# A transformer encoder layer on one Trainium2 core: the order of fetches, stores and operand loads in branch B

## The chip, the cores and the metric

The kernel runs on one core of a Trainium2 chip. Its engines work side by side, each through its own list of instructions in order: TensorE (PE; its weight loads are shown as PEld), VectorE (DVE), ScalarE (ACT), GpSimd (POOL) and SyncE (SP). SyncE does nothing but issue transfers (DMAs); ScalarE and GpSimd issue some too. An instruction that has to wait holds up everything behind it in its engine's list. The metric is the device time in microseconds (us) of one execution, the median over several runs. Before the change it is 2152.05 us (2150.76 to 2152.45, three runs).

## The reference

One encoder layer with two token mixers in parallel, on two sequences: a prompt of 1024 tokens and a sample of 512, model width 1024, all in 32-bit floats.

```python
xn = rmsnorm(x)
z  = xn @ W_in        # q_A k_A v_A | q_B k_B v_B | gate_A gate_B
o_A = gqa_attention(rope(norm(q_A)), rope(norm(k_A)), v_A)     # 8 heads, 2 kv heads
o_B = neighbourhood_attention(q_B, k_B, v_B, bias)             # 8 heads, 8 x 16 window on a grid
mix = (sigmoid(gate_A) * (o_A @ W_pA) + sigmoid(gate_B) * (o_B @ W_pB)) @ W_out
x = x + mix
x = x + relu(rmsnorm(x) @ W_up)**2 @ W_down
y = rmsnorm(x)
```

Tokens lie on a grid that is 64 wide. In branch B a query sees a window of 8 rows by 16 columns, with a learned bias for each relative position.

## The kernel before

**Numbers.** Each matrix product is done as three (helper `mm3`): an operand is split into a high part `hi`, rounded to the matmul's format, and a low part `lo = x - hi`, and hi*hi + hi*lo + lo*hi are summed. So a loaded operand first goes through a *split* (`split`, L192 and on): a copy on ScalarE for `hi` (L199), a subtraction on VectorE for `lo` (L206).

**Stages.** The sample (512 tokens, `NB` = 1) goes through the token mixer first, then the prompt (1024 tokens, `NB` = 2), then both through the MLP. A mixer has branch A (attention), branch B (`phB`, L905 and on) and phase G, which projects branch B and applies W_out. The *long branch B* is that of the prompt; in the profile it lies between 776 and 1070 us.

**Branch B in units.** A unit is one head and one quarter of the grid's columns: 8 heads x 4 = `n` = 32 units. The loop at L1166 runs over `i`; in iteration `i` it traces

- `s_unit` of unit `i`: scores on TensorE (`sb`), bias and row minimum on VectorE (L1031), exp on ScalarE into a tile `pb` (L1057, two such tiles in the long branch), the scaling on GpSimd (L1060). Between sums and exp it traces `turn` of unit `i-1`;
- the loads for later: `prep_bias` (L926), `prep_v` (L935; *strips* of the value matrix, `vs`), `load_qk` (L245);
- in iterations with `i % 8` = 6 and 7 the projection `qkproj` of the next two heads, which is evacuated by L971 and L973 (`qB`) and L991 and L993 (`kB`);
- five or eight steps of other TensorE work (`fill.pull`): at first the products of gate B (`gate`, L433), later projection A (`proj_a`, L867);
- `t_unit` of the unit three behind and `v_unit` of the unit four behind.

**The detour.** The probabilities have to be transposed before the product with the values. In the first 24 units of the long branch (`moved`) TensorE doesn't do it. `turn` (L1064) transposes 32 x 32 blocks on VectorE (L1069), GpSimd stores the tile to memory (`tb<-pb`, L1071), and `fetch_t` (L1073) has SyncE fetch it back with the blocks in their new places (`bh<-tb`, L1080, four transfers a unit, three `bh` tiles in turn). `t_unit` splits the fetched tile (ScalarE L1091, VectorE L1092), and `v_unit` (L1112) multiplies it with the strips (`ob`); `finish_o` copies the result out (L464, L465, L478) and puts it into memory (`obd`). Other units are transposed by TensorE (L1101).

**Gates.** `gate` computes 16 tiles in the long branch B, each of eight steps. A tanh on ScalarE (L454) writes one of two buffers `sg`, and a store takes it to memory (`zg`, L455). `store[0]` is ScalarE's queue; in the long branch B it is SyncE's.

**Projection A.** `proj_a` loads the first weights and the output of branch A (`load_o`: `rawo`, L846; three raw buffers) and leaves their splits in the list `oa_held`, from which the loop takes them. The weights go to a slot that the inputs `x` occupy until their last use.

**What sets the order.** The kernel is written for a planner that gives each engine its list. It starts from the order in which the program traces the instructions and from its own model of when each is ready, gives tiles their places and adds all waits. `keep_in_program_order` pins an instruction behind the one traced before it on its engine; all matmuls of the long branch B are pinned so. `note` remembers an instruction, and a block under `behind` puts what it traces behind those remembered on that engine: the score sums behind splits on VectorE, the exps behind splits on ScalarE, the fetches and strips behind loads on SyncE. The block empties the list.

Of the kernel before, what the change touches and what calls it, by code (L numbers as in the profile page):

```python
# [11 lines left out]
F32 = mybir.dt.float32  # L12
# [6 lines left out]
P = 128  # L19
# [42 lines left out]
def encoder(ctx: ExitStack, tc: tile.TileContext, xs, outs, w):  # L62
# [123 lines left out]
    def note(engine, op):  # L186
        if held_pe:
            firm[engine].append(op.ins)
# [230 lines left out]
    def run(tr, nxt, first):  # L419
# [7 lines left out]
        oad = dram.tile([4 * P, T], F32, name=f"oad{N}")  # L427
        obd = dram.tile([4 * P, T], F32, name=f"obd{N}")
        fill = Fill()
        store = [nc.scalar]  # L430
        later_put = []

        def gate(goff, dst, c0=0, c1=NC8):  # L433

            nxt_w = load_cols(win, goff + c0 * P, P, f"g{N}_{goff}_{c0}")
            yield
            for c in range(c0, c1):
                wg = nxt_w
                held = []
                if c + 1 < c1:  # L440
                    nxt_w = load_cols(win, goff + (c + 1) * P, P, f"g{N}_{goff}_{c + 1}", hold=held)
                for tb in range(NB):
                    nm = f"{N}_{goff}_{c}_{tb}"
                    g_ = mm(f"gps{nm}")
                    for k in range(NC8):
                        mm3(g_, wg[k][0], wg[k][1], xh(tb, k), xl(tb, k), k == 0, k == NC8 - 1)
                        if k + 1 < NC8:
                            yield
                        if k == 2:
                            while held:  # L450
# [3 lines left out]
                    nc.scalar.activation(sg, g_, AF.Tanh, scale=0.5)  # L454
                    store[0].dma_start(dst[c * P : (c + 1) * P, tb * 512 : tb * 512 + 512], sg)  # L455
                    yield

        def finish_o(o, n, dst, pool, nm, parts=None):

            t = pool.tile([HD, 512], F32, tag="ot", name=f"ot_{nm}", bufs=1)  # L460
            if len(o.shape) == 3:

                tv = t[:, : 2 * n].rearrange("p (i q) -> p i q", i=2)
                nc.scalar.activation(tv, o[HD:P], AF.Copy)  # L464
# [4 lines left out]
            n_os = 2  # L469
            if parts is not None:  # L470
                hi, lo, ps = parts
                b = pool.tile([P, n], F32, tag="os", name=f"os_{nm}", bufs=n_os)[ps, :n]
# [4 lines left out]
            b = pool.tile([HD, n], F32, tag="os", name=f"os_{nm}", bufs=n_os)  # L477
            nc.vector.tensor_tensor(b[:, :n], o[0:HD, :n], t[:, :n], op=ALU.add)  # L478
            if store[0] is nc.scalar:
                nc.scalar.dma_start(dst, b[:, :n])  # L480
            else:
                later_put.append((dst, b[:, :n]))


        def load_a(g, between=None, then=None, last=None):
# [353 lines left out]
        def load_o(br, hold=None, raw_of=raw_tile):  # L839
            parts = []  # L840
            for k in range(4 - br):
                t = slot([P, 2, T], F32R, f"oX{N}_{br}_{k}", first and br + k == 0)

                def ask(k=k, t=t):
                    raw = raw_of(f"rawo{N}_{br}_{k}")
                    note("SP", nc.sync.dma_start(raw[:, :T], (oad, obd)[br][k * P : (k + 1) * P, :]))  # L846
                    return partial(split, t[:, 0, :], t[:, 1, :], raw[:, :T])

                if hold is None:
                    ask()()  # L850
                elif NB == 1 or k < 2:
                    hold.append(ask())
                else:

                    cuts = []
                    early = hold[k - 2]

                    def then(early=early, ask=ask, cuts=cuts):
                        early()
                        cuts.append(ask())  # L860
# [45 lines left out]
        with phase(f"phB{N}") as ph:  # L906
# [41 lines left out]
            def qkproj(pr, wqk, dest):  # L948
# [4 lines left out]
                for tb in range(NB):  # L953
                    cs = slice(tb * 512, tb * 512 + 512)
                    pq = mm(f"pqb{N}_{pr}_{tb}")
                    for k in range(NC8):
                        mm3(pq, wq[k][0], wq[k][1], xh(tb, k), xl(tb, k), k == 0, k == NC8 - 1)
                        yield
                    for e in range(2):
                        hs = slice(64 * e, 64 * e + 64)  # L960
                        ls = slice(64 - 64 * e, 128 - 64 * e)

                        src = pq[hs].rearrange("p (r j c) -> p j r c", j=4, c=16)

                        def strip_view(s_):
                            return qT[s_, e, :].rearrange("p (j r c) -> p j r c", j=4, c=16)[
                                :, :, tb * 8 : tb * 8 + 8, :
                            ]

                        dst_h, dst_l = strip_view(hs), strip_view(ls)  # L970
                        nc.scalar.activation(dst_h, src, AF.Copy, scale=0.125)  # L971
                        for jj in range(4):
                            nc.vector.scalar_tensor_tensor(  # L973
                                dst_l[:, jj],
                                src[:, jj],
                                0.125,
                                dst_h[:, jj].bitcast(F32),
                                op0=ALU.mult,
                                op1=ALU.subtract,
                            )  # L980
# [174 lines left out]
            qp = None  # L1155
            held = []
            if moved:
                store[0] = nc.sync
                held_pe.append(1)
                fill.pull(3)  # L1160
            due_t, due_v = {}, {}
            for i, u in enumerate(units):
                ls = 3 if u in moved else 3 - NB
                due_t.setdefault(i + ls, []).append(u)
                due_v.setdefault(i + ls + 1, []).append(u)
            for i in range(n + 4 - NB):  # L1166
                if i < n - 8:
                    f = (5 if i < 2 else 2 + i % 2) if NB == 1 else 5 - (i % 6 == 5)
                else:
                    f = 3 + i % 2 if NB == 1 else 8  # L1170
                if NB == 2 and i == n - 10:
                    pa = proj_a(ph, raw_here)
                    next(pa)
                if i < n:
                    late = i > 0 and units[i - 1] in moved
                    s_unit(units[i], partial(turn, units[i - 1]) if late else None)
                    h, j = units[i]
                    if j == 1 and h < 7:
                        if moved:
# [40 lines left out]
                fill.pull(f - f // 2)  # L1220
                for u in due_v.get(i, ()):
                    v_unit(u)
                if 0 < i <= n and units[i - 1] in moved:
                    fetch_t(units[i - 1])
                if NB == 2 and oa_held and i >= n - 9:
                    oa_held.pop(0)()
                while len(later_put) > (i < n):
                    nc.sync.dma_start(*later_put.pop(0))
            fill.drain()
            held_pe.clear()  # L1230


        mgs = {}
# [713 lines left out]
```

## Time and profile before

| | |
|---|---|
| median of 3 runs | 2152.05 us |
| profiled execution | 2149.47 us |
| its span, first to last instruction | 2147.7 us |
| mean granted clock of TensorE | 0.995 |
| TensorE busy | 2104.3 us (98%) |
| VectorE busy | 1486.6 us (69%) |
| ScalarE busy | 1141.4 us (53%) |
| GpSimd busy | 368.6 us (17%) |
| long branch B, 776 to 1070 us: TensorE busy | 279.88 of 294.00 us, clock 0.98 |

The profile lists instructions by kernel line, engine and tile name, as `out<-in`. A view of waits says who waited for whom: total, number, longest. The chain of waits follows the last instruction back to what released it; "issue" there is idle time for which the profile shows no cause. A timeline row has start, duration, engine, line, operation, and in brackets the idle time before it with what ended it. In rows by stage stand, behind the length, the busy time of PE, PEld, DVE, ACT and POOL with the number of instructions, then the granted clock (1.00 is full), the share of the DMA engines' time in use, and GB/s.

### The profile page before, as it was taken

The numbers are of one execution on the slowest core, as the hardware profiler recorded it, in microseconds if no ns is written. First come the engines' busy times: TensorE is split into PE (matmuls) and PEld (weight loads), VectorE is DVE, ScalarE is ACT, GpSimd is POOL, SyncE is SP. The second block draws the span as 40 slices with busy tenths as digits, with TensorE's granted clock in tenths as the row PEclk, the third lists the DMA queues.
The fourth block names the chain that finished last, engine by engine and source line by source line (L and its number), as shares of the span: only waits on it lengthen the run. The fifth ranks groups of instructions, "written<-read, shape, count | busy, mean of one in ns | idle before, by whom it ended". The sixth has DMA issues, their size and how long they took to land.

```text
span 2147.7 us, 32028 instructions
## 1 busy us (share of the span) xinstructions
PE 2104.3 (98%) x10871; PEld 1840.9 (86%) x10871; DVE 1486.6 (69%) x2793; ACT 1141.4 (53%) x2487; POOL 368.6 (17%) x470
## 2 busy tenths in 40 slices
PE   9999999999999999989999999999999999999998
PEld 8888778888897888777888899999999988888886
DVE  6665786767657757766882877778777777759662
ACT  6664653767656645544540566566655643334442
POOL 2232310323232214533200200003000000000000
PEclk9999999999999999999999999999999999999999
DMA  6437557520122136667572665578545799788561
GB/s 192 131 101 209 154 151 251 185 77 25 52 81 70 42 96 191 202 187 205 174 235 103 210 199 178 177 245 206 164 142 157 253 356 342 215 271 282 167 206 59
DMA packets 337002, 372.95 MB, mean 174 GB/s; under 512 B 33471, under 2 KB 269639, under 8 KB 336839
## 3 DMA queue, kind: packets, MB, share of 16 engines
q1 hardware_dynamic: 296695, 296.17, 44.6%
q10 hardware_dynamic: 31072, 45.11, 6.0%
q0 software_dynamic: 9072, 29.63, 4.7%
q8 instruction: 86, 1.41, 0.3%
q14 instruction: 77, 0.63, 0.1%
HBM read 274.29 MB, written 97.32 MB: 173 GB/s over the span
## 4 chain that ended last, share of the span: by engine, by line
PE 65%; issue 1%; DVE 1%; DMA 1%; ACT 1%; POOL 0%; SPq 0%; POOLq 0%; ACTq 0%; DVEq 0%
PE dn L212 20%; PE ua L212 6%; PE ud L212 6%; PE uc L212 6%; PE gpss L212 5%; PE ops L212 4%; PE ub L212 3%; PE pqbs L212 2%; PE ppbs L212 2%; PE pkbs L212 2%; PE dnf L212 2%; PE ppas L212 1%; PE pTs L812 1%; PE obs L212 1%; PE sbs L212 1%
## 5 line engine op out<-in xcount | busy, mean ns | idle before, releaser
L212 PE MATMUL dn<-wd,ah 128*128 128x512 f32 x1248 | 384.3, 389 | 0.0
L212 PEld LDWEIGHTS dn<-wd,ah 128*128 128x128 f32 x1248 | 234.3, 188 | 48.4
L212 PE MATMUL dn<-wd,al 128*128 128x512 f32 x624 | 242.9, 389 | 0.0
L1421 ACT ACTIVATE ah<-ar 128x512 fp32r<-128x512 f32 x168 | 104.1, 627 | 196.6 <-PE dn L212 179.8
L212 PE MATMUL gpss<-xs_0h,w_gs 128*128 128x512 f32 x512 | 188.5, 402 | 0.7 <-DVE ot_Bs L465 0.4
L1422 DVE TENSOR_TENSOR al<-ar,ah 128x512 fp32r<-128x512 f32 x168 | 114.0, 687 | 74.3 <-ACT ah L1421 66.3
L212 PE MATMUL ud<-B,A 128*128 128x384 f32 x768 | 143.6, 335 | 0.7 <-DVE c L1539 0.7
L212 PE MATMUL uc<-B,A 128*128 128x384 f32 x768 | 143.7, 334 | 0.0
L212 PE MATMUL ua<-B,A 128*128 128x384 f32 x768 | 138.8, 334 | 0.0
L212 PEld LDWEIGHTS dn<-wd,al 128*128 128x128 f32 x624 | 117.2, 188 | 24.4
L778 POOL TENSOR_SCALAR ps<-ps,rls 128x1024 f32<-128x1024 f32 (+1 forms) x96 | 96.8, 1009 | 225.7 <-DVE rls L777 200.3
L212 PEld LDWEIGHTS ud<-B,A 128*128 128x128 f32 x768 | 133.9, 188 | 1.1 <-DVE c L1539 1.1
L212 PEld LDWEIGHTS uc<-B,A 128*128 128x128 f32 x768 | 134.1, 188 | 0.2 <-ACT A L1421 0.2
L212 PEld LDWEIGHTS ua<-B,A 128*128 128x128 f32 x768 | 133.7, 188 | 0.2
L818 DVE TENSOR_TENSOR ptls<-pTs,pths 128x512 fp32r<-128x512 f32 x160 | 107.7, 687 | 37.6 <-ACT pths L817 36.6
L817 ACT ACTIVATE pths<-pTs 128x512 fp32r<-128x512 f32 x160 | 94.1, 597 | 73.8 <-PE pTs L812 71.5
L212 PE MATMUL ops<-wh_os,mgs 128*128 128x512 f32 x384 | 119.4, 391 | 0.0
L772 DVE TENSOR_REDUCE nms<-ss 128x1 f32<-128x1024 f32 (+1 forms) x96 | 99.9, 1041 | 25.7 <-PE ss L770 25.1
L212 PEld LDWEIGHTS gpss<-xs_0h,w_gs 128*128 128x128 f32 x512 | 96.2, 189 | 18.8 <-DVE w_gs L206 0.7
L180 POOL TENSOR_TENSOR rs_f<-ms_f,mhalf 128x1 f32<-128x1 f32 x6 | 4.0, 666 | 590.7 <-DVE ms_f L176 590.7
L775 ACT ACTIVATE ps<-ss,nms 128x1024 f32<-128x1024 f32 (+1 forms) x96 | 93.2, 971 | 22.9 <-DVE nms L772 20.4
L812 PEld LDWEIGHTS pTs<-ident,ps 128*128 128x128 f32 x640 | 78.0, 140 | 28.4 <-POOL ps L778 4.3
(288 smaller groups left out, 5158.1 us busy)
## 6 DMA issues: line engine op xcount, KB each, us to landing
ar<-ud SPq DMA_DIRECT2D x120, 512.0 KB, 4.6
br<-in_w_mlp_down_dram SPq DMA_DIRECT2D x72, 512.0 KB, 5.4
rawu<-in_w_mlp_up_dram SPq DMA_DIRECT2D x64, 512.0 KB, 4.1
ud<-c ACTq DMA_DIRECT2D x128, 192.0 KB, 2.9
raw_gs<-in_w_in_dram SPq DMA_DIRECT2D x32, 512.0 KB, 3.9
ud<-cs SPq DMA_DIRECT2D x64, 192.0 KB
tbs<-pbs POOLq DMA_DIRECT2D x24, 384.0 KB, 3.5
bhs<-tbs SPq DMA_DIRECT2D x96, 96.0 KB, 2.2
```

What stands on the lines that cost most here:

```text
L180: nc.gpsimd.tensor_tensor(r[:, :n], m[:, :n], mhalf[:, :n], op=ALU.pow)
L212: op = nc.tensor.matmul(out, a, b, **kw)
L772: nc.vector.tensor_reduce(nm_, s, axis=AX.X, op=ALU.max, negate=True)
L775: nc.scalar.activation(p, s, AF.Exp, bias=nm_, accum_out=l)
L778: nc.gpsimd.tensor_scalar(p, p, rl, 1.0, op0=ALU.mult, op1=ALU.mult)
L812: nc.tensor.transpose(pt[:, j * P : (j + 1) * P], PP[u, j][:, kc * P : (kc + 1) * P], ident)
L817: nc.scalar.activation(hi, pt, AF.Copy)
L818: nc.vector.tensor_tensor(lo, pt, hi.bitcast(F32), op=ALU.subtract)
L1421: nc.scalar.activation(hi, src, AF.Copy)
L1422: nc.vector.tensor_tensor(lo, src, hi.bitcast(F32), op=ALU.subtract)
```

## The change

All of it lies in the token mixer. The stores of gate tiles and of branch B's outputs go through one function, `put`. Where `slot_no[0]` is None it issues the store on ScalarE's queue at once, as before. In the long branch B it notes the store with the number of the unit, and the loop issues it on SyncE at the end of the next unit. Before, gate stores were issued on SyncE where the tanh is traced, and of the outputs' stores the loop always kept the latest one back.

The fetch of a moved unit is traced after the scores of the unit two behind it, ahead of that iteration's strips; before, it stood at the end of the iteration that turns it, ahead of the output store.

The evacuations of `qkproj` for `qB` are noted, so sums and exps that are traced later stand behind them.

`proj_a` is begun at iteration 21 in place of 22 in the long branch; the second of the two places that take a split begins at 22 in place of 23, the first stays at 23. In the short branch the splits are taken from iteration 21 on, in place of 23. `load_o` asks for its raw tile ahead of the slot for the split.

```diff
-        store = [nc.scalar]
-        later_put = []
+        later_put, slot_no = [], [None]
+
+        def put(dst, src):
+            if slot_no[0] is None:
+                nc.scalar.dma_start(dst, src)
+            else:
+                later_put.append((slot_no[0], dst, src))
...
-                    store[0].dma_start(dst[c * P : (c + 1) * P, tb * 512 : tb * 512 + 512], sg)
+                    put(dst[c * P : (c + 1) * P, tb * 512 : tb * 512 + 512], sg)
...
-            if store[0] is nc.scalar:
-                nc.scalar.dma_start(dst, b[:, :n])
-            else:
-                later_put.append((dst, b[:, :n]))
+            put(dst, b[:, :n])
...
             for k in range(4 - br):
+                raw = None
+
+                def ask(k=k):
+                    r = raw_of(f"rawo{N}_{br}_{k}")
+                    note("SP", nc.sync.dma_start(r[:, :T], (oad, obd)[br][k * P : (k + 1) * P, :]))
+                    return r
+
+                now = hold is None or NB == 1 or k < 2
+                if now:
+                    raw = ask()
                 t = slot([P, 2, T], F32R, f"oX{N}_{br}_{k}", first and br + k == 0)
...
-                        nc.scalar.activation(dst_h, src, AF.Copy, scale=0.125)
+                        note("ACT", nc.scalar.activation(dst_h, src, AF.Copy, scale=0.125))
                         for jj in range(4):
-                            nc.vector.scalar_tensor_tensor(
+                            op = nc.vector.scalar_tensor_tensor(
...
+                            note("DVE", op)
...
             if moved:
-                store[0] = nc.sync
+                slot_no[0] = 0
...
             for i in range(n + 4 - NB):
+                if moved:
+                    slot_no[0] = i
...
-                if NB == 2 and i == n - 10:
+                if NB == 2 and i == n - 11:
                     pa = proj_a(ph, raw_here)
                     next(pa)
                 if i < n:
                     late = i > 0 and units[i - 1] in moved
                     s_unit(units[i], partial(turn, units[i - 1]) if late else None)
+                    if i > 1 and units[i - 2] in moved:
+                        fetch_t(units[i - 2])
...
-                if oa_held and i >= n - 9:
+                if oa_held and i >= (n - 9 if NB == 2 else n - 11):
                     oa_held.pop(0)()
...
-                if 0 < i <= n and units[i - 1] in moved:
-                    fetch_t(units[i - 1])
-                if NB == 2 and oa_held and i >= n - 9:
+                if NB == 2 and oa_held and i >= n - 10:
                     oa_held.pop(0)()
-                while len(later_put) > (i < n):
-                    nc.sync.dma_start(*later_put.pop(0))
+                while later_put and later_put[0][0] < i:
+                    nc.sync.dma_start(*later_put.pop(0)[1:])
             fill.drain()
             held_pe.clear()
+            slot_no[0] = None
+            for _, dst, src in later_put:
+                nc.sync.dma_start(dst, src)
```

More of the change, by code (lines that the diff above doesn't have):

```diff
@@ L468, in finish_o @@
                 nc.scalar.activation(t[:, :n], o[HD:P, :n], AF.Copy)
-            n_os = 2
             if parts is not None:
                 hi, lo, ps = parts
-                b = pool.tile([P, n], F32, tag="os", name=f"os_{nm}", bufs=n_os)[ps, :n]
+                b = pool.tile([P, n], F32, tag="os", name=f"os_{nm}", bufs=2)[ps, :n]
                 nc.vector.tensor_tensor(b, o[0:HD, :n], t[:, :n], op=ALU.add)
@@ L476, in finish_o @@
                 return
-            b = pool.tile([HD, n], F32, tag="os", name=f"os_{nm}", bufs=n_os)
+            b = pool.tile([HD, n], F32, tag="os", name=f"os_{nm}", bufs=2)
             nc.vector.tensor_tensor(b[:, :n], o[0:HD, :n], t[:, :n], op=ALU.add)
-            if store[0] is nc.scalar:
-                nc.scalar.dma_start(dst, b[:, :n])
-            else:
-                later_put.append((dst, b[:, :n]))
+            put(dst, b[:, :n])
         def load_a(g, between=None, then=None, last=None):
@@ L841, in load_o @@
             for k in range(4 - br):
+                raw = None
[6 more added lines that the diff above has]
+                    raw = ask()
                 t = slot([P, 2, T], F32R, f"oX{N}_{br}_{k}", first and br + k == 0)
[L844 to L847, printed above, removed]
+                cut = partial(split, t[:, 0, :], t[:, 1, :])
                 if hold is None:
-                    ask()()
-                elif NB == 1 or k < 2:
-                    hold.append(ask())
+                    cut(raw[:, :T])
+                elif now:
+                    hold.append(partial(cut, raw[:, :T]))
                 else:
@@ L856, in load_o, with then @@
                     early = hold[k - 2]
-                    def then(early=early, ask=ask, cuts=cuts):
+                    def then(early=early, ask=ask, cut=cut, cuts=cuts):
                         early()
-                        cuts.append(ask())
+                        cuts.append(partial(cut, ask()[:, :T]))
                     hold[k - 2] = then
```

## The prediction, made before the changed kernel ran

> **What bounds the kernel now.** I read the page first, then busy time by stage, then the waits of TensorE alone, the chain of waits, the clock in short windows, and last the queues that feed the places found.
>
> ```profile
> span 2147.7 us, 32028 instructions
> PE 2104.3 (98%) x10871; PEld 1840.9 (86%) x10871; DVE 1486.6 (69%) x2793; ACT 1141.4 (53%) x2487; POOL 368.6 (17%) x470
> ```
>
> TensorE is the bound. A change that moves other engines' work can only win where TensorE stands still or runs slowly. The change touches the neighbourhood attention (branch B) of both sequences, above all the long one, which runs from 776 to 1070 us.
>
> ```profile
> 890.00:960.00 70.00, 60.99 (x279) 50.74 (x278) 42.69 (x100) 31.71 (x62) 24.49 (x33) 0.95 0.65 189
> 960.00:1000.00 40.00, 40.00 (x194) 34.10 (x193) 29.64 (x73) 21.20 (x43) 16.93 (x23) 1.00 0.73 215
> 1000.00:1012.00 12.00, 8.62 (x27) 5.77 (x26) 8.27 (x19) 8.21 (x14) 4.22 (x4) 0.72 0.57 172
> ```
>
> The first figures are the stretch, its length and TensorE's busy time; the third from the end is the granted clock. Idle are 70.00-60.99 = 9.0 us in the first row, nothing in the second, and 12.00-8.62 = 3.4 in the third; where it idles the clock falls below 1 as well. TensorE's waits from 900 to 1010 us name the places:
>
> ```profile
> PE obs L212 <- issue: 5.5, 3, 3.2
> PE pqbs L212 <- DVE qBs L973: 3.5, 1, 3.5
> PE ppas L212 <- ACT oXs L199: 1.7, 1, 1.7
> PE ppas L212 <- DVE oXs L206: 1.6, 2, 1.2
> ```
>
> ```profile
> 943.20 3.24 issue
> ...
> 952.89 1.78 issue
> ```
>
> Place A is the 3.5 us of a projection (pqbs) at 904. Place B is 3.24 us before the value product obs at 943.20; place C is the other two waits of obs, 1.78 at 952.89 and 5.5-3.24-1.78 = 0.48. Place D is projection A (ppas) at 1001, 1.7+1.6 = 3.3 us, whose operand oX is not split yet. Each idle may also cost clock (columns as before):
>
> ```profile
> 908.48:911.90 3.42, 3.42 (x9) 2.66 (x9) 2.75 (x8) 1.69 (x4) 2.63 (x4) 0.50 0.65 179
> 946.03:949.45 3.42, 3.01 (x11) 3.04 (x12) 1.44 (x5) 1.35 (x5) 1.23 (x2) 0.50 0.85 274
> 952.86:956.27 3.41, 1.63 (x12) 1.63 (x12) 2.62 (x4) 2.61 (x4) 0.00 (x0) 1.00 1.05 275
> 1000.65:1004.06 3.41, 1.20 (x4) 0.47 (x3) 2.22 (x4) 3.39 (x5) 0.00 (x0) 1.00 0.37 110
> 1004.06:1010.88 6.82, 5.65 (x16) 3.85 (x16) 4.93 (x14) 3.54 (x9) 4.22 (x4) 0.50 0.63 191
> ```
>
> Behind A, B and D the clock is halved for 3.42, 3.42 and 6.82 us; work done in them takes twice as long, so half of the busy time there is lost: 3.42/2 = 1.7, 3.01/2 = 1.5, 5.65/2 = 2.8. The window with 3.41-1.20 = 2.21 us idle is followed by a halved one, C's own, with 3.41-1.63 = 1.78, isn't slowed, nor does the clock fall behind it. With its clock each place costs: A 3.5+1.7 = 5.2, B 3.24+1.5 = 4.7, C 2.26, D 3.3+2.8 = 6.1; 18.3 us in all, which is what there is to win.
>
> **The change part by part.** No instruction or transfer is added or dropped. It moves 96 fetches, 16 gate stores, the obd stores and some splits, and it adds order edges.
>
> *Gate stores and fetches.* SyncE issues in order. Its own waits between 800 and 1000 us, and what it did around 915:
>
> ```profile
> SPq L1080 <- DMA tbs<-pbs: 36.4, 15, 4.4
> SPq L455 <- ACT sgs L454: 23.7, 3, 14.4
> SPq L1080 <- PE obs L212: 10.5, 3, 6.2
> ```
>
> ```profile
> 924.18 0.34 SPq L455 DMA_DIRECT2D zgs<-sgs  x1
> 924.57 0.43 SPq L245 DMA_DIRECT2D raw_gs<-in_w_in_dram  x1
> 925.17 2.38 SPq L1080 DMA_DIRECT2D bhs<-tbs  x4
> 927.65 0.45 SPq L1228 DMA_DIRECT2D obds<-os_Bs  x1
> ```
>
> ```profile
> 909.76 0.57 POOL L1071 DMA_DIRECT2D tbs<-pbs  x1 [0.19 <-DVE rlbs L1059]
> ```
>
> ```profile
> DMA to landing us min/median/max: 2.6/3.5/6.6
> ```
>
> The last row is of the tbs stores. The block stored at 909.76 had landed by 909.76+6.6 = 916.4 at the latest, but its fetch went out at 925.17: a gate store sat in front of it, waiting 14.4 us for a tanh. Behind the fetch sat the obd store. What that does to B and C, on ScalarE and on VectorE:
>
> ```profile
> 940.89 0.62 ACT L1057 ACTIVATE pbs<-sbss,nmbs 128x384 f32<-128x384 f32 x1 [4.33 <-DMA tbs<-pbs]
> ...
> 942.72 0.84 ACT L1091 ACTIVATE bhs<-bhs 128x768 fp32r<-128x768 f32 x1
> ...
> 952.25 0.60 ACT L454 ACTIVATE sgs<-gpss 128x512 f32<-128x512 f32 x1 [4.85 <-PE gpss L212]
> 952.75 0.83 ACT L1091 ACTIVATE bhs<-bhs 128x768 fp32r<-128x768 f32 x1
> ```
>
> ```profile
> 933.07 0.42 DVE L478 TENSOR_TENSOR os_Bs<-ot_Bs 64x256 f32<-64x256 f32 x1 [2.44 <-DMA obds<-os_Bs]
> ```
>
> VectorE waits 2.44 us at 933.07 for an obd store to free its buffer. That holds up the score sums, so the turned block, so its landing, so the exp at 940.89 by 4.33 us; the split of the fetched block (L1091) comes only at 942.72, and that is B. In C the next split stands behind a tanh (4.85 us), which waits for TensorE, which has just come out of B.
>
> After the change a gate store is traced at the end of the unit behind its tanh, the obd store ahead of the fetch, and the fetch at the head of the next unit. In the stretch above nothing is left before the fetch that waits for TensorE: it can go at 916.4 instead of 925.17, 8.8 us sooner, and the obd store sooner still. That is more than B's 3.24 and the 4.33 behind it. I take B and C as gone: 4.7+2.26 = 7.0 us, between 0 (the split stays behind a tanh) and 7.0. Where the detour runs at its pace nothing is gained or lost by the later tracing, since the fetch waits for its store's landing there (36.4 us over 15 waits) in either order.
>
> What the move is charged with: the four fetches of a unit now stand ahead of its four strips (vss).
>
> ```profile
> 875.34 1.73 SPq L1080 DMA_DIRECT2D bhs<-tbs  x4
> ...
> 880.97 1.73 SPq L1080 DMA_DIRECT2D bhs<-tbs  x4
> ```
>
> The strips come later by 1.73 us of issue and the wait for the landing (4.4 at most), 6.1 together. A strip is used four units after its own, and a unit is 880.97-875.34 = 5.6 us here, so 22 us of other units' work cover it; without the cover it would be 6.1 us once, since all later ones are shifted alike. A gate store that is one unit late keeps one of two tanh buffers 5.6 us longer. The loop pulls five steps a unit and a gate tile has eight, so tanh come every 1.6 units and a buffer is asked for again after 3.2, 18 us; I charge nothing. Without that cover the next tanh would wait up to a unit.
>
> *Order edges.* The projection's evacuations (L971, L973) are now noted, so that sums and exps traced behind them are also issued behind them. A waits for exactly such an evacuation (L973). Gain between 0 and A's 5.2; or a loss, where a sum is held back, as large as one more wait like A's 3.5. No row shows an evacuation held up by a later exp alone, so I take 0.
>
> *Projection A's operands.* The loads are asked for one unit sooner in the long sequence, and the last splits come a unit sooner (in the short one, two).
>
> ```profile
> 991.38 1.73 SPq L1080 DMA_DIRECT2D bhs<-tbs  x4
> 993.22 0.36 SPq L846 DMA_DIRECT2D rawos<-oads  x1
> ```
>
> ```profile
> 1001.71 1.99 ACT L199 ACTIVATE oXs<-rawos 128x1024 fp32r<-128x1024 f32 x2
> ```
>
> The fourth load goes out at 993.22, behind a fetch that held SyncE up to 6.2 us for a buffer (the row of L1080 and obs above), and the splits run at 1001.71, just when TensorE wants them. A split is 1.0 us of ScalarE, which is busy 21.2 of the 40.0 us from 960 to 1000, so three fit ahead of D. Gain between 0 and 6.1, or a loss of 1.0 where a split that comes early holds up an exp. The last of four stays closest to its use, so I leave the longest wait for VectorE's part, 1.2, standing and take 6.1-1.2 = 4.9, clock included, since 1.2 is below the 1.78 that cost no clock.
>
> *The rest of the plan.* Order on every engine is worked out anew from the traced order, so small waits move. In the first sequence, where the splits come two units sooner, TensorE's longest wait in branch B is this:
>
> ```profile
> PE obs L212 <- ACT ot_Bs L464: 3.0, 1, 3.0
> ```
>
> Bounds are one wait like its 3.0 gone, and one like A's 3.5 new. I charge 1.0.
>
> **Sum.** -7.0 -4.9 +0 +1.0 = -10.9 us against the profiled execution, 2149.47 us (1.8 outside the span). The median of the runs is 2152.05, 2.6 above it; from there 2152.05-10.9 = 2141.
>
> **Rivals.**
>
> *All four places go* (0.14): A too, nothing new: 2152.05-18.3 = 2134. For: the new edges stand on the line that A waits for. Against: an edge that holds back sums and exps doesn't move the evacuation ahead of the other work in front of it, the splits of fetched blocks among it.
>
> *Only one of the two parts works* (0.14): B and C go and D's splits queue behind a tanh, 2152.05-7.0 = 2145; or only D, 2147.
>
> *D's halved clock stays* (0.04), since it hangs on something else than D's short gaps: D gives only 3.3-1.2 = 2.1 and the time is 2152.05-7.0-2.1+1.0 = 2144. Against: the window of 2.21 idle stands right before it. The Trainium skill, page "TensorE: Matmul & The Clock Gate", section "Why this matters for your kernels", has a rule of this kind: only gaps above some 3 us drop the clock. D's gaps are 1.7 at most and the clock fell all the same, so the trace disagrees with it taken as a matter of single gaps.
>
> *The change does not do what it says* (0.12): the planner issues by its own estimate of readiness, fetch and gate store end up where they were or the wait moves from one to the other; within 4 us of 2152.
>
> *Slower: the split behind the tanh becomes the rule* (0.16). A fetch traced in the later unit may be planned as landing late, and the split L1091 then goes behind that unit's tanh on ScalarE, as at 952.25, where TensorE paid 1.78 us. Sixteen gate tiles run beside the detour. From 10.9/1.78 = 6 of them on the gain is spent; ten give 2152.05-10.9+17.8 = 2159. For: the two rows at 952. Against: one of sixteen does it now, and there TensorE had just come out of B.
>
> **How the numbers follow.** The forecast has 0.40: B, C and most of D. With 0.2% (4.3 us, about what a measurement of this kernel can tell from no change) as the bound, faster holds the forecast, the full case, the half case and that of the clock, 0.72; same 0.12; slower 0.16. The range goes down to 2132, where the full case ends with 2 us of the first sequence, and up to 2154, which takes in no change and leaves out most of the slower case.
>
> **What would show it.** SyncE's wait for tanh (23.7) near 0, and the fetch after 909 out by about 916: right on the first part. TensorE's 5.5 us for obs gone and the clock at 1.00 from 940 to 960: right on B and C. Projection A with under 1.5 us of wait for oX and no halved clock at its start: right on D. A still there shows the edges idle. I am wrong if obs waits appear in many units with a tanh ahead of L1091, or if the strips become what obs waits for.

## The result, and the profile after

The changed kernel takes 2143.3 us (median of 6 runs, 2140.93 to 2144.53), the kernel before on the same chip 2150.51 (6 runs, 2148.93 to 2152.45). The ratio is 0.9964, with a 95% interval of 0.9951 to 0.9977. That is 7.7 us faster (7.2 by the medians), where 10.9 were forecast. The profiled execution took 2144.53 us, 4.9 less than the profiled one before; its span, 2142.7 us, is 5.0 shorter.

Busy time by stage for the same three stretches as before (length, then busy PE, PEld, DVE, ACT, POOL with counts, granted clock, DMA share, GB/s):

```profile
890.00:960.00 70.00, 62.48 (x289) 52.59 (x288) 44.58 (x107) 34.58 (x68) 28.29 (x38) 0.95 0.67 201
960.00:1000.00 40.00, 38.18 (x175) 32.11 (x175) 27.49 (x69) 19.19 (x38) 13.66 (x20) 0.96 0.67 189
1000.00:1012.00 12.00, 9.41 (x42) 6.76 (x41) 10.39 (x21) 7.14 (x13) 5.36 (x4) 1.00 0.51 150
```

The first stretch, which held A, B and C, idles 7.5 us (9.0 before) at the same clock of 0.95. The second, which had no idle at all, now has 1.8 and a lower clock. In the third the clock is back at 1.00. TensorE's waits from 900 to 1010 us (engine, tile, line, releaser; total, number, longest):

```profile
PE obs L212 <- issue: 6.8, 2, 4.7
PE sbs L212 <- DVE kBs L1001: 1.8, 1, 1.8
PE pqbs L212 <- DVE ot_Bs L471: 0.7, 1, 0.7
PE ppas L212 <- ACT oXs L199: 0.6, 1, 0.6
PE ppas L212 <- DVE oXs L206: 0.5, 2, 0.2
```

Against before, A has gone from 3.5 to 0.7 and D from 3.3 to 1.1, but the waits of obs (B and C) have gone from 5.5 up to 6.8, and a wait of 1.8 for kB is new. Of the three waits of obs, the first has grown from 0.48 to 2.1 and B from 3.24 to 4.7; C's 1.78 is gone. The granted clock, in its own windows:

```profile
942.30:949.13 6.83, 5.82 (x18) 5.18 (x19) 3.26 (x6) 1.84 (x4) 0.74 (x2) 0.50 0.80 226
986.68:990.09 3.41, 1.59 (x10) 1.27 (x9) 3.36 (x10) 2.21 (x6) 3.08 (x5) 1.00 0.07 29
990.09:993.50 3.41, 3.41 (x10) 2.82 (x10) 3.32 (x8) 2.40 (x6) 1.02 (x2) 0.50 0.55 171
```

Two spells of halved clock are left of three: one of 6.83 us behind B (it was 3.42) and one of 3.41 behind the new wait. Those behind A and D are gone.

**The fetches did go out sooner.** SyncE's list of after, then TensorE's, then SyncE's list of before for the next block:

```profile
918.26 1.97 SPq L1088 DMA_DIRECT2D bhs<-tbs  x4
...
926.34 1.73 SPq L1088 DMA_DIRECT2D bhs<-tbs  x4
```

```profile
917.30 0.89 PE L212 MATMUL obs<-bhs,vss 128*128 128x256 f32 x6
```

```profile
934.99 1.73 SPq L1080 DMA_DIRECT2D bhs<-tbs  x4
```

The fetch that went out at 925.17 before goes out at 918.26, the moment the obs at 917.30 ends (918.19): it waits for the `bh` tile which that product reads, one of three used in turn. The next fetch, that of the block which B's product reads, goes out at 926.34 in place of 934.99, 8.7 us sooner. B stays all the same, as the lists of ScalarE, GpSimd, VectorE and TensorE show:

```profile
935.99 0.62 ACT L1065 ACTIVATE pbs<-sbss,nmbs 128x384 f32<-128x384 f32 x1 [0.70 <-DMA tbs<-pbs]
...
937.33 0.60 ACT L460 ACTIVATE sgs<-gpss 128x512 f32<-128x512 f32 x1
940.77 0.61 ACT L1065 ACTIVATE pbs<-sbss,nmbs 128x384 f32<-128x384 f32 x1 [2.85 <-DMA tbs<-pbs]
...
941.39 0.83 ACT L1099 ACTIVATE bhs<-bhs 128x768 fp32r<-128x768 f32 x1
```

```profile
934.30 3.15 POOL L1019 TENSOR_TENSOR bms<-rects,msks 128x384 f32<-128x384 f32 x2
937.40 0.57 POOL L1079 DMA_DIRECT2D tbs<-pbs  x1
```

```profile
928.86 1.29 DVE L206 TENSOR_TENSOR w_gs<-raw_gs,w_gs 128x512 fp32r<-128x512 f32 x2 [0.27 <-ACT w_gs L199]
...
931.02 0.97 DVE L1077 STREAM_TRANSPOSE pbs<-pbs 128x768 f32<-128x768 f32 x1
...
932.23 1.09 DVE L1100 TENSOR_TENSOR bhs<-bhs 128x768 fp32r<-128x768 f32 x1
...
942.25 0.96 DVE L1100 TENSOR_TENSOR bhs<-bhs 128x768 fp32r<-128x768 f32 x1 [0.57 <-ACT bhs L1099]
```

```profile
943.31 1.62 PE L212 MATMUL obs<-bhs,vss 128*128 128x256 f32 x6 [4.68 <-issue]
```

B's product starts 0.1 us after the subtraction of its split (942.25 + 0.96 = 943.21), so it is the split that it waits for. The exp that held this split before (940.89, idle 4.33) now comes at 935.99, idle 0.70; counted from the start of the long branch, it is the 37th in both kernels. So far the change does what was forecast. But in ScalarE's list the split (L1099, 941.39) no longer stands behind that exp and a tanh alone: the planner has put the first exp of the next unit, the 39th (940.77), ahead of it. That exp waits for its `pb` tile until the store of an earlier block has landed, and that store left GpSimd at 937.40, behind the making of a bias tile (`bm`), which takes 3.15 us for its two halves. The row of the page on these fetches has a median of 2.2 us from issue to landing:

```profile
bhs<-tbs SPq DMA_DIRECT2D x96, 96.0 KB, 2.2
```

So the block was there by about 926.34 + 1.73 + 2.2 = 930.3 and lay for 11 us, at the end of which its split waited for another block's store. Ahead of that, the 2.1 us before obs at 933.5 have the same form on VectorE: the subtraction L1100 stands behind a weight split and a transposition.

### The profile page after: what moved, and what is told of

Same layout as the page of the kernel before. It is cut to its first block, busy times and chain, and to the rows that moved or that the text cites. A ratio compares the mean times of both kernels' runs of the same rounds, so it can differ in the third digit from the quotient of the medians.

```text
span 2142.7 us, 32014 instructions
## 1 busy us (share of the span) xinstructions
PE 2102.9 (98%) x10871; PEld 1841.3 (86%) x10871; DVE 1484.2 (69%) x2793; ACT 1141.0 (53%) x2487; POOL 374.0 (17%) x470
## 4 chain that ended last, share of the span: by engine, by line
PE 52%; DVE 1%; issue 0%; DMA 0%; ACT 0%; SPq 0%; POOLq 0%; POOL 0%; ACTq 0%; DVEq 0%
PE dn L212 20%; PE ua L212 6%; PE ud L212 6%; PE uc L212 6%; PE ops L212 4%; PE ub L212 3%; PE ppbs L212 2%; PE ppas L212 2%; PE dnf L212 2%; PE pt L353 0%; PE obs L212 0%; PE gpss L212 0%; PE sbs L212 0%; PE ptbs L1109 0%; DVE A L1435 0%
## 5 line engine op out<-in xcount | busy, mean ns | idle before, releaser
L780 POOL TENSOR_SCALAR ps<-ps,rls 128x1024 f32<-128x1024 f32 (+1 forms) x96 | 96.9, 1010 | 225.7 <-DVE rls L779 200.4
```

Of the source, the lines that this page charges most:

```text
L780: nc.gpsimd.tensor_scalar(p, p, rl, 1.0, op0=ALU.mult, op1=ALU.mult)
```

## The experiments

Places are named as in the prediction; times are medians, ratios are against the kernel before on the same chip, with 95% intervals.

| kernel | us | ratio |
|---|---|---|
| operands of projection A alone | 2147.75 | 0.9985 (0.9976 to 0.9994) |
| order edges of qB alone | 2150.32 | 1.0002 (0.9993 to 1.0011) |
| store lag alone | 2145.99 | 0.9981 (0.9972 to 0.9990) |
| moved fetches alone | 2147.32 | 0.9988 (0.9979 to 0.9997) |
| store lag and moved fetches | 2145.00 | 0.9974 (0.9963 to 0.9985) |
| the whole change | 2143.30 | 0.9964 (0.9951 to 0.9977) |
| whole change, four `bh` tiles | 2158.59 | 1.0043 (1.0030 to 1.0057) |
| whole change, split ahead of later exps and sums | 2138.53 | 0.9948 (0.9936 to 0.9961) |
| the same on ScalarE alone | 2140.23 | 0.9953 (0.9939 to 0.9967) |
| the same, split traced earlier | 2142.73 | 0.9971 (0.9961 to 0.9982) |
| the same, kB's evacuations noted too | 2140.17 | 0.9948 (0.9936 to 0.9961) |
| kernel before, split ahead of exps and sums | 2153.07 | 1.0007 (0.9998 to 1.0015) |

Within these intervals the parts add up: 0.9985 x 1.0002 x 0.9974 = 0.9961, the whole 0.9964.

### Projection A's operands alone

The new `load_o`, and the iterations:

```diff
-                if NB == 2 and i == n - 10:
+                if NB == 2 and i == n - 11:
...
-                if oa_held and i >= n - 9:
+                if oa_held and i >= (n - 9 if NB == 2 else n - 11):
...
-                if NB == 2 and oa_held and i >= n - 9:
+                if NB == 2 and oa_held and i >= n - 10:
```

> The kernel before with the third part alone: projection A's loads and splits sooner, nothing else. As predicted (the splits of oX came too late, and D's idle halves the clock): TensorE's wait for oX falls from 3.3 us to under 1.5, no halved clock at projection A's start, time 4 to 6 us below the kernel before. Rival (D's halved clock hangs on something else): the wait falls, the clock stays halved, 2 us. A, B and C stay as before (3.5 us and 5.5 us of wait) by both.

TensorE's waits from 890 to 1015 us:

```profile
PE pqbs L212 <- DVE qBs L978: 3.5, 1, 3.5
PE sbs L212 <- DVE kBs L998: 1.8, 1, 1.8
...
PE ppas L212 <- DVE oXs L206: 0.5, 2, 0.2
PE ppas L212 <- ACT oXs L199: 0.3, 1, 0.3
```

D's waits for oX fall from 3.3 to 0.8 and the clock from 1000 to 1012 is 1.00 (0.72 before): this part mends D by itself. It also makes the 1.8 us for kB, at once and alone, and that is one reason why it brings 3.2 us (by the ratio) and not the 4 to 6 expected. The rows of after show how: the weight split of projection A (985.55), two sums and a transposition stand ahead of kB's subtraction on VectorE.

```profile
985.55 0.76 DVE L206 TENSOR_TENSOR w_pas<-raw_pas,w_pas 128x256 fp32r<-128x256 f32 x2 [1.80 <-ACT w_pas L199]
...
988.39 1.36 DVE L1001 TENSOR_TENSOR kBs<-pkbs,kBs 64x512 fp32r<-64x512 f32 x2
```

### The order edges alone

```diff
-                        nc.scalar.activation(dst_h, src, AF.Copy, scale=0.125)
+                        note("ACT", nc.scalar.activation(dst_h, src, AF.Copy, scale=0.125))
```

and the same for the subtraction on VectorE.

> The kernel before with the second part alone: the evacuations of the branch B queries noted, so that later sums and exps stand behind them. As predicted (the edges are idle): A stays at 3.5 us with its halved clock, time within 2 us of the kernel before. Rival (A fell from 3.5 to 0.7 us in the changed kernel because of the edges): A under 1 us, no halved clock behind it, time 4 to 5 us below. B and C are not touched by either.

```profile
PE pqbs L212 <- DVE qBs L973: 3.4, 1, 3.4
PE sbs L212 <- DVE nmbs L1032: 2.6, 1, 2.6
```

The edges leave A's wait where it was, 3.4 us, and the time too. Another one appears, 2.6 us for the sums. Against the expectation A has no halved clock behind it here; the last section returns to that.

### Stores alone, fetches alone, both

The store lag is `put` with `slot_no` (the diff above). The moved fetches are:

```diff
                     s_unit(units[i], partial(turn, units[i - 1]) if late else None)
+                    if i > 1 and units[i - 2] in moved:
+                        fetch_t(units[i - 2])
...
-                if 0 < i <= n and units[i - 1] in moved:
-                    fetch_t(units[i - 1])
```

> The kernel before with the lag of the gate stores (and obd stores) alone; fetches stay at the end of the unit. The run with stores and fetches together won 5.8 us and lost A's 3.5 us of wait with its clock. If the stores did that: A under 1 us, time 4 to 6 us below the kernel before, obs waits still 5 to 7 us. If the fetches did: A at 3.5 us, time within 2 us of the kernel before.

> The kernel before with the fetches a unit later and ahead of the strips alone; gate stores stay where the tanh is. If the fetches made A's gain: A under 1 us, 4 to 6 us below. If the stores made it: A at 3.5 us and the same time. SyncE's wait for tanh stays above 15 us in either case; if it held up the fetch by itself, obs waits would be at 5.5 us or more, and the fetch near 925 would go right behind the gate store.

> The kernel before with the first part alone: gate stores one unit behind, fetches traced a unit later ahead of the strips. As predicted (the gate store ahead of the fetch makes B and C): waits for obs under 1 us, clock full from 930 to 955, time 6 to 8 us below the kernel before. Rival (the fetch is held by the third fetched tile, which the product obs three units back frees only after the projection, whatever stands before it on SyncE, and the split waits behind an exp): the fetch of the block stored near 909 us goes out when that obs ends, obs waits stay at 5 to 7 us with a halved clock, time within 2 us of the kernel before.

With the stores alone, SyncE and TensorE around the fetch that went out at 925.17 before:

```profile
911.19 0.64 SPq L245 DMA_DIRECT2D raw_gs<-in_w_in_dram  x1
926.87 1.75 SPq L1082 DMA_DIRECT2D bhs<-tbs  x4
```

```profile
925.95 0.89 PE L212 MATMUL obs<-bhs,vss 128*128 128x256 f32 x6
```

No gate store is in front of the fetch any more, and it still goes out at 926.87, 0.03 us after the end of obs (925.95 + 0.89 = 926.84). The tile held it; the gate store, which stood in front before, hid that. A stays in this kernel (4.2 us). With the fetches alone, and with both, A falls to the same 0.7 as in the changed kernel. So A hangs on where the fetch is traced. The times don't follow A alone: the stores gain 4 us with A as it was, where at most 2 had been expected, and the fetches only 2.6 with A gone, where 4 to 6 had been. Before, ScalarE copied obs out at 906.03, behind a kB copy that waited for the scores; in the changed kernel it does so at 901.50, ahead of the kB copies (902.21), and the projection begins 0.7 us after the scores:

```profile
904.07 0.59 ACT L991 ACTIVATE kBs<-pkbs 64x512 fp32r<-64x512 f32 x1 [2.96 <-PE sbs L212]
...
906.03 0.59 ACT L464 ACTIVATE ot_Bs<-obs 64x512 f32<-64x512 f32 x1
```

```profile
901.50 0.59 ACT L470 ACTIVATE ot_Bs<-obs 64x512 f32<-64x512 f32 x1 [2.52 <-PE obs L212]
```

What in the planner's reckoning turns these two round was not followed further. The waits of obs (5.5 us before) are gone in none of the three kernels: 2.7 with the stores alone, 3.5 + 1.7 = 5.2 with the fetches alone, 6.6 with both. So of the gain forecast at B and C the stores alone give about half, the fetches alone next to nothing (and a new wait of 3.2 us for sums), and together they give none. ScalarE's lists show what goes with it: with either part alone the split of B's block stays ahead of the 39th exp (942.95 against 946.12, 940.32 against 941.65), and with both it falls behind it (944.55 against 943.93), as in the changed kernel. Why the planner does so was not followed.

### Four tiles for the fetched blocks

```diff
-bufs=3)
+bufs=4)
```

for `bh`. Room for it comes from the long branch's bias tiles (`bm`, four to two), `za` (two to one) and small tiles (`sml`, eight to six).

> The changed kernel with a fourth fetched tile (room taken from bias tiles, 4 to 2 in the long branch, one za tile, small tiles 8 to 6). If the third tile, freed by the product obs, is what holds the fetch of the block stored near 909: it goes out at its landing, about 915, in place of 918.3. If that late fetch also made the obs waits, they fall by about 3 of 6.8 us and the time by 3 to 5 us; if the splits stand behind other work, the waits stay within 1 us and the time within 3 us of the changed kernel.

```profile
918.55 1.86 SPq L1088 DMA_DIRECT2D bhs<-tbs  x4
```

```profile
921.02 0.89 PE L212 MATMUL obs<-bhs,vss 128*128 128x256 f32 x6
```

```profile
PE obs L212 <- issue: 6.4, 2, 4.3
```

The fetch now leaves 3.4 us before that obs ends (921.91), where three tiles let it leave only after. The waits of obs are 6.4 us, 6.8 without. So neither this fetch nor the third tile is what B waits for. (B's own block is the next one; its fetch goes out behind the landing of its store with four tiles as with three.) The 15 us that this kernel loses against the changed one come with the room taken from the other tiles; which of these costs them was not separated.

### The split ahead of later exps and sums

On the changed kernel, the split of a fetched block is noted, so exps and sums traced later stand behind it on their engine:

```diff
-                    nc.scalar.activation(hi, lo.bitcast(F32), AF.Copy)
-                    nc.vector.tensor_tensor(lo, lo.bitcast(F32), hi.bitcast(F32), op=ALU.subtract)
+                    note("ACT", nc.scalar.activation(hi, lo.bitcast(F32), AF.Copy))
+                    note("DVE", nc.vector.tensor_tensor(lo, lo.bitcast(F32), hi.bitcast(F32), op=ALU.subtract))
```

> The changed kernel, with the splits of the fetched blocks noted too, so that the exps and sums traced behind a split are issued behind it. If B's 4.7 us in the changed kernel is a split that stands behind an exp on ScalarE, which itself waits for a stored tile to land: obs waits fall from 6.8 us to under 2, no halved clock near 942, time 6 to 9 us below the changed kernel, near 2135. If the block itself comes too late (fetch or landing): the waits stay, and exps wait behind the split as well, time the same or up to 5 us longer.

```profile
PE sbs L212 <- DVE nmbs L1039: 2.9, 1, 2.9
PE obs L212 <- issue: 2.1, 1, 2.1
```

B's 4.7 us and its 6.83 us of halved clock are gone, and of the three spells before one of 3.41 us is left. The split now runs at 935.89, ahead of the 39th exp at 939.16. So the place of the split in the lists was the cause of B. A wait of 2.9 us for sums takes part of it back. This kernel, at 2138.53 us, is clearly faster than the kernel before (0.9948). Against the changed kernel it is 4.8 us by the medians and 3.4 by the ratios; the intervals of the two overlap, but the kernel with the edge on ScalarE alone (0.9953) and the one with kB noted too (0.9948), both told of below, lie on the same side.

The same edge on ScalarE alone (the first of the two lines):

> The changed kernel with the split noted on ScalarE alone (L1099), not on VectorE (L1100). In the changed kernel the 4.68 us before obs had the split behind an exp on ScalarE, and the 2.14 us before that the subtraction behind a weight split, sums and a transposition on VectorE. If ScalarE's order is what counts, the 4.68 us are gone as with both notes and the time is about 2138.5; if VectorE's counts, it is nearer to 2143.3, that of the changed kernel.

```profile
PE obs L212 <- issue: 5.3, 2, 3.2
```

B's wait falls only from 4.7 to 3.2, with 3.4 us of halved clock, and no wait for sums appears; the time, 2140.23, can't be told from that with both. On ScalarE the split is ahead of the 39th exp (937.37 against 940.46), but on VectorE its subtraction (939.67) stands behind a transposition that first waits 0.7 us for GpSimd. So both engines' lists hold the split back.

The edge on both, and the split traced at the head of its unit:

```diff
+                    for u in due_t.get(i, ()):
+                        if u in moved:
+                            t_unit(u)
```

(ahead of the unit's scores, and left out further down)

> The kernel with the splits noted (2138.5), and the split of a fetched block traced at the head of the unit, ahead of that unit's sums and exps, in place of its middle. If the 2.14 us of obs that were left are the split's subtraction standing behind sums and the block transposition on VectorE: that wait is gone, time 2 to 4 us below, near 2135.5. If exps now wait for fetches that land late: score or obs waits appear elsewhere, 0 to 10 us above 2138.5.

```profile
PE sbs L212 <- DVE nmbs L1039: 3.8, 1, 3.8
```

That goes too far: the sums are now 3.8 us late, obs still waits 3.0 us, and the time is 2142.73.

The edge on both, and kB's evacuations (L999, L1001) noted too:

> The changed kernel with the split noted on both engines, and the evacuations of the projection for kB (L999, L1001) noted as well. The 1.82 us before the scores at 988 come from VectorE: the split of projection A's weights, two sums and a transposition stand ahead of kB's subtraction. If the edge moves those sums behind it, the 1.82 us go and the time is about 2138.5 - 1.8 = 2137; if it is the weight split that holds it up, or the sums so delayed become the next wait, it stays at 2138.5 or gets 1 to 3 us slower.

kB's 1.8 us stay: on VectorE the weight split (980.86), two sums and the transposition keep their place ahead of kB's subtraction (983.71). The edge acts on sums and exps alone, so it can't move the other two, and these sums were traced ahead of kB's evacuation.

### The same edge on the kernel before

> The kernel before, with one thing added: the splits of fetched blocks (L1091, L1092) are noted, so that sums and exps traced behind them are also issued behind them; nothing of the change is in it. If B and C hang on the place of the split in ScalarE's list, and not on when the fetch goes out, the order edge should work here too: B's 3.24 us before obs goes to under 1 with its halved clock, A and D stay, and the time is about 2150.5 - 4.7 = 2146. If the edge only helps together with the moved fetches, stores or operand loads, the 3.24 us stay or come back as a wait for sums, and the time is 2150 +- 2.

```profile
PE sbs L212 <- DVE nmbs L1031: 4.4, 1, 4.4
...
PE obs L212 <- issue: 3.4, 2, 1.8
```

```profile
956.15 1.06 ACT L199 ACTIVATE w_gs<-raw_gs 128x1024 fp32r<-128x1024 f32 x1 [5.20 <-DMA raw_gs<-in_w_in_dram]
```

B's wait falls by half here too, from 3.2 to 1.6 (the two of obs are now 1.6 and 1.8), with no halved clock behind it, but the next sums come 4.4 us late, behind a weight split for which ScalarE waits 5.2 us. What B gains here it gains on VectorE, where the subtraction (941.38) now goes ahead of the sums and the transposition. On ScalarE the edge has nothing to move: in the kernel before the split stands ahead of the 39th exp already, and the 37th, which still waits 4.2 us for a landing, is traced ahead of the split. (In the changed kernel that exp comes early, idle 0.70, so there the place of the split counts.) The load of the weight for which ScalarE waits went out at 949.72 on SyncE; in the changed kernel with the edge it went out at 944.71, and the wait for sums is 2.9. In the kernel before the edge is worth nothing, 1.0007 (the profile is of the fastest of its executions, 2148.11 us), and on the changed kernel 3 to 5 us. That the rest of the difference lies in how early SyncE gets to the weight loads fits the two rows, but was not tried by itself.

## Why the prediction was right and wrong

The time, 2143.3, lies within the range, 2.3 us from the forecast; the steps do not come out so well. Each against the profiled executions, a halved clock counted as half of the busy time in it:

| step | forecast | profiled |
|---|---|---|
| B and C | -7.0 | 7.0 before; 6.8 + 5.82/2 = 9.7 after: +2.7 |
| D | -4.9 | 6.1 before; 1.1 after: -5.0 |
| order edges, A | 0 | 5.2 before; 0.7 after: -4.5 |
| rest of the plan | +1.0 | kB 1.8 + 3.41/2 = 3.5 and w_pa 1.5 new, first sequence -1.9: +3.1 |
| sum | -10.9 | -3.7 |

The span is 5.0 shorter, so 1.3 lies in smaller waits, not followed one by one. The rows of the table aren't independent. TensorE stands ready for B's product 4.6 us sooner than before (at 943.31 - 4.68 = 938.63, before at 943.20), mostly because A and the first sequence's wait are gone, and the product starts 3.1 us sooner (946.44 before). So the 1.4 us by which B's wait has grown are gain from there handed on, and no new loss. Two rows on which the last step rests, both of after, from 900 to 1015 us and from 200 to 400:

```profile
PE ppas L212 <- DVE w_pas L206: 1.5, 1, 1.5
```

```profile
PE obs L212 <- DVE bhs L1117: 1.1, 1, 1.1
```

The first sequence's longest wait in branch B (3.0 before) is now the 1.1 of the second row.

**The step that failed** is "That is more than B's 3.24 and the 4.33 behind it. I take B and C as gone". It took the earlier fetch and output store as enough, and left the split where it stood in ScalarE's list. Half of that chain held: VectorE's wait of 2.44 us for the output store is gone, the store for which the 37th exp waits leaves 4.6 us sooner (932.44, before 937.00), and that exp comes 4.9 us sooner. But the lists were drawn up anew, and the split went behind the 39th exp, which waits 2.85 us for the next store. So the split came only 1.3 us sooner (941.39, before 942.72), and B stayed. The kernels with the noted split show it: with the split ahead of that exp, and its subtraction ahead of the transposition, B is gone.

Nor was the fetch at 925.17 that of B's block. The block stored at 909.76 is read by the obs at 938.08, which waited 0.48 us. B's block was stored and fetched later in the kernel before (the second row is SyncE's wait from 934 to 936 us):

```profile
928.21 0.59 POOL L1071 DMA_DIRECT2D tbs<-pbs  x1 [2.70 <-DVE rlbs L1059]
```

```profile
SPq L1080 <- DMA tbs<-pbs: 2.2, 1, 2.2
```

Its fetch at 934.99 waited for its own store to land, and not for a gate store. The block was there by about 934.99 + 1.73 + 2.2 = 938.9, four microseconds before its split at 942.72, and of that the prediction took no note. That this fetch came 8.7 us sooner, close to the 8.8 worked out for the other block, is chance.

Within that step, "nothing is left before the fetch that waits for TensorE: it can go at 916.4" was wrong by 1.9 us (918.26). The fetch itself waits for TensorE, by its tile. In the kernel before, the obs that frees this tile ended at 923.50 + 0.89 = 924.39, so without the gate store the fetch could have gone only 0.8 us sooner. It goes 6.9 us sooner in the changed kernel because that obs does (918.19); with the stores alone, where A stays, it goes no sooner at all (926.87). The row of the waits for obs at L1080 (10.5 us, three times) was quoted there and used only for projection A's loads.

For C the number came out, its 1.78 us is gone, but again by a change of order: the split, which stood behind the tanh at 952.25, now goes ahead of it (945.46 against 950.41).

**Order edges 0** was right, by the kernel with the edges alone (3.4 us left, 1.0002). "A still there shows the edges idle" was a bad test, for A went by another part, the moved fetches. The part on the fetches had no word on A.

**D** was right in mechanism and size: the forecast left 1.2 us at full clock, there are 1.1. The operands alone show it is this part's doing. In the changed kernel another 1.5 us for the weights of the same projection comes new and stands under the rest.

**Rest of the plan, +1.0** was too small. The bounds given, one wait of 3.0 gone and one like A's 3.5 new, were both met, together with a further 1.5. The new wait for kB belongs to the operands' part: the loss bounded there at 1.0, "where a split that comes early holds up an exp", came on VectorE instead, as a weight split ahead of an evacuation, at 3.5 with its clock.

**Of the rivals**, that the split behind other work becomes the rule came nearest to what happened at B, but at two places and not ten, and with an exp or a weight split in front, not a tanh. That the planner goes by its own estimate was true of the split, which it moved, and not of the fetch and the gate store that this rival named. The half case named 2147 for "only D"; D alone (the operands) measured 2147.75. So close a match is luck, for that 2147.75 includes the new wait for kB. What the whole has beyond D is first of all A, for which the case "all four go" had argued from the edges.

**Strips and late gate stores**, charged at nothing: strips are not among what obs waits for after. SyncE's wait for tanh fell from 23.7 us to 9.8, and to nothing for the fetch at 918.26:

```profile
SPq L1238 <- ACT sgs L460: 9.8, 3, 5.8
```

## What to carry to other kernels

Before an earlier transfer is credited with a wait, find the transfer that feeds this very instruction and look when it landed; if it lay there for microseconds, the wait belongs to the order in the list of the engine that reads it, and an order edge is what helps. Where a planner draws up the lists anew, a place in a list that a forecast rests on has to be pinned, or charged as open. Where a wait in front of a transfer is taken away, look for the next one it has, the free tile above all. And a total that comes out right says little about its terms: here a loss of 2.7 where 7.0 had been expected as gain was covered by 4.5 gained elsewhere. Part of that loss is the same 4.5 handed on, for time gained at one place is waited out again at the next if what feeds that place stays late.

## What the runs showed of the hardware

The clock doesn't follow the length of a wait, but how it falls on windows of 3.41 us. A's wait was 3.50 us before, with 3.42 us of halved clock behind it; 3.5 with the operands alone, with 6.83 behind it; and 3.44 with the edges alone, with none. Stretches of the kernel with the edges alone, and of the changed kernel with the split ahead (its 2.9 us wait lies across the two):

```profile
903.18:906.59 3.41, 1.81 (x12) 1.44 (x10) 1.06 (x2) 1.54 (x3) 1.33 (x2) 1.00 0.35 135
906.59:910.00 3.41, 1.57 (x7) 1.34 (x8) 3.35 (x11) 2.00 (x4) 0.44 (x1) 1.00 0.57 158
```

```profile
947.15:950.56 3.41, 2.21 (x13) 1.77 (x11) 1.03 (x3) 1.54 (x2) 0.00 (x0) 1.00 0.96 273
950.56:953.97 3.41, 1.73 (x8) 1.58 (x9) 3.33 (x10) 2.17 (x6) 0.57 (x1) 1.00 0.93 277
```

The windows idle 1.60 and 1.84 us in the first, 1.20 and 1.68 in the second, and the clock stays at 1.00 (there is no spell of halved clock behind either). The new wait for kB in the changed kernel is only 1.8 us, but lies in one window (3.41 - 1.59 = 1.82 idle), and the next is halved. Over all windows at full clock between 300 and 2100 us, in the thirteen profiles of this case (windows counted in steps of 3.41 us from the start of a halved spell), up to 1.54 us idle was never followed by a halved window, 1.92 or more always; in between, about half the window, it went either way. A window already halved was followed by another from 0.79 us idle on, and by a full one up to 0.54. So the same wait can cost its own length alone, or half of the busy time in a halved spell on top: 1.7 us for a full one of 3.41, 2.9 for the 6.83 behind B. The prediction's 1.7 for A's clock held for one alignment only. The Trainium skill, page "TensorE: Matmul & The Clock Gate", Part 1, has windows of this length that run free of the kernel, and the trace agrees: between 300 and 2100 us every halved spell of these profiles is 3.41 or 6.83 us long, and they fall differently in each run. Its advice in "Why this matters for your kernels", to leave no gaps above some 3 us, doesn't hold here as a rule for single gaps: 3.44 us in one gap cost no clock, 1.82 did.
